# A two-layer decoder trunk on one core: block sums' VectorE steps behind the low parts of probabilities, strided pairs that begin with the first sum

## The chip, the cores and the metric

The kernel runs on one core of a Trainium2 chip. The metric is device time in microseconds (us) for one execution of the whole program; lower is better. The engines are named as the profile names them: PE is TensorE, DVE is VectorE, ACT is ScalarE, POOL is GpSimd, and SP issues the DMAs.

## The reference

Two layers over a sequence of 1024 tokens with 1024 channels, in fp32. Each layer normalises x to h, projects h with one combined matrix, runs two attentions, gates and merges them, and then a gated feed-forward part with a short convolution.

```python
for l in range(DEPTH):                                    # DEPTH = 2
    h = rmsnorm(x, norm1[l])
    ...  # h @ w_in[l]: q, k, v of 12 dilated heads and 4 stick-breaking heads, two gates
    # mixer A, groups (window, dilation) = (128, 1), (512, 4), (2048, 16), 4 heads each:
    scores = einsum('brhnqc,brhnkc->brhnqk', qs, kw) * hd**-0.5 + bias      # ALiBi, causal window
    p = exp(scores - max(scores)); o = einsum('...qk,...kc->...qc', p, vw) / sum(p)
    # mixer B: stick-breaking attention in log space
    x = x + (gate_a * (A @ w_br_a) + gate_b * (B @ w_br_b)) @ w_o[l]
    # then x = x + conv-gated FFN(rmsnorm(x, norm2[l]))
```

## The kernel before, in words

**Two parts for one fp32 value.** Matmuls run on a high and a low part of each operand. `split(hi, lo, src)` casts on ACT (the high part, L129 in the profile) and subtracts on DVE (the low part, L130). A product of two such values is three matmuls: high by high, high by low, low by high. For attention probabilities, `parts` (called with p0, p1 or sb) makes p0h and p0l, with a raised priority in the scheduler. `apply` (L729) multiplies first p0h, then p0l, with v.

**Strided pairs.** Fourteen times per layer, two column blocks of w_in that feed dilated heads and gates (128 columns each) are multiplied with h by Strassen's scheme: fewer block products, of sums of blocks. The halves of h are `H[n][part]`, and `half(n, k)` is four 128x512 blocks of them. Four sums of such blocks are made once per layer: S[1], S[2], S[3] and S[4], each in two parts (t_hi, t_lo; the fourth in the place of a half of h itself, as hh and hl). `block_sums` makes the list of their steps. `first` makes block i of a sum on POOL in three steps (L928, L929, L930); `further` turns the first sum's block into the second's, or that into the fourth's, with two DVE steps (L937, L938); `in_two` splits a block. All sums of one kind pass through one buffer, h_sum, block by block. So the next sum's block i can only be written when the one before it has been split.

A pair's program is `pair_rest.run`. It adds and subtracts the raw blocks of weights on POOL (L1031, L1034, L1037, L1038), makes two parts of each (`piece`: w_hi on ACT, w_lo on DVE), and runs the five remaining products with `seven`, twelve matmuls of 128x512 each (L905 to L907). The other two are run earlier in `ahead`; ACT copies the first of them out of its PSUM bank as q1s (L1000), and SP keeps it in memory, from where it is loaded as u. The five products are w6·S[2], w5·S[1], w7·S[3], w3·half(0,1) and w4·S[4]. They are summed in two PSUM banks, i_a (`pa`) and i_c (`pc`), in the order pa, pc, pa, pc, pa; the two names change banks from pair to pair. A product with `first=False` adds onto what its bank holds. After each product DVE adds the bank to a result u or u5 (L1051, L1056, L1064, L1069, L1077), and this read must be done before the next product is added to the same bank.

**What sets the order.** A queue object `dense` hands out matmuls of dense products between the attention's matmuls at a rate per attention item. Block sums are side jobs: `plan(after, steps)` lists them with the names that must be done (N01s, N11s: the scores of an attention item; plain, 01, v0: products), and `aside` runs one at a time. Before the first strided pair all side jobs left are flushed. Within an engine the order is fixed when the program is built; a scheduler with priorities decides it from the order and the priority in which the code issues.

Of the kernel before, what the change touches and what calls it, by code (L numbers as in the profile page):

```python
# [11 lines left out]
ALU = mybir.AluOpType  # L12
# [30 lines left out]
AHEAD_B = 3  # L43
X_AT = (3, 5, 7, 9)
AHEAD = 200


def f32(ap):
    return ap.bitcast(F32)
# [3 lines left out]
def trunk_kernel(ctx, tc, x, norm1, w_in, b_gate, w_br, w_o, norm2, w_up, conv_w, conv_b, w_down, norm_f, out, depth=None, probe=None):  # L53
    nc = tc.nc
    act, dve, pe, pool = nc.scalar, nc.vector, nc.tensor, nc.gpsimd
# [60 lines left out]
    def bank(tag, name):  # L116
        return ps.tile([P, 512], F32, tag=tag, name=name)
# [9 lines left out]

    def split(hi, lo, src):
        act.copy(hi, src)  # L129
        dve.tensor_tensor(lo, src, f32(hi), ALU.subtract)  # L130


    def weights(src, cols, place=None):
# [61 lines left out]
    class Dense:  # L195
# [30 lines left out]
        def at(self, ahead, f):  # L226
            self.later.setdefault(self.count + ahead, []).append(f)
# [26 lines left out]
        def step(self):  # L254
            while True:
                if self.now is None:
                    self.now, self.nxt = self.nxt or self.choose(), None
                    if self.now is None:
                        return bool(self.later) and self.share()
                    self.ready(self.now, READY)  # L260
                    if self.now[2] and not self.started:
                        while self.side:
                            n = len(self.side)
                            self.aside()
                            assert len(self.side) < n, (self.side, self.done)
# [165 lines left out]
    S, B = {}, {}  # L431
# [161 lines left out]
    def parts(src, n, name):  # L593

        hi, lo = small(name + "h", F32R), small(name + "l", F32R)
        with tc.high_priority(offset=AHEAD):
            split(hi[:, :n], lo[:, :n], src[:, :n])
        return hi, lo

    def fold(dst, o):  # L600
# [310 lines left out]
    def block_sums(made):  # L911


        keep = {"o": made} if made is not None else {}
        S.clear()

        def at(t, i):
            if t == 3 and i < 2:
                if "o" not in keep:
                    keep["o"] = sb.tile([P, 2, HF], F32, tag="ot", name="h_sum2")  # L920
                return keep["o"][:, i, :]
            if "r" not in keep:
                keep["r"] = quarter("h_sum")
            return keep["r"][:, i, :]

        def first(t, a, b, i):
            r, (ah, al), (bh, bl) = at(t, i), a()[i], b()[i]
            pool.tensor_tensor(r, f32(al), f32(bl), ALU.subtract)  # L928
            pool.tensor_tensor(r, r, f32(ah), ALU.add)  # L929
            pool.tensor_tensor(r, r, f32(bh), ALU.subtract)  # L930

        def further(t, a, i):
            if t == 4:

                S[4] = half(0, 0)
            r, (ah, al) = keep["r"][:, i, :], a()[i]
            dve.tensor_tensor(r, f32(ah), r, ALU.subtract)  # L937
            dve.tensor_tensor(r, r, f32(al), ALU.add)  # L938

        def in_two(t, i):  # L940
            if t not in S:
                new_s(t)
            split(*S[t][i], at(t, i))

        b11, b12, b21, b22 = (lambda n=n, k=k: half(n, k) for k in range(2) for n in (1, 0))
        todo = []

        def plan(after, steps):

            for k in range(max(steps) + 1):  # L950
                todo.append((after, lambda fs=steps.get(k, ()): [g() for g in fs]))

        def series(after, t, f, lag, gap):
            steps = {}
            for i in range(4):
                steps.setdefault(i * gap, []).append(lambda i=i: f(i))
                steps.setdefault(i * gap + lag, []).append(lambda i=i: in_two(t, i))
            plan(after, steps)

        def third(i):  # L960
            return lambda: first(3, b22, b12, i)

        def cast(i):
            return lambda: in_two(3, i)

        if made is None:
            plan({"B14"}, {0: [third(0)], 6: [third(1)]})
        plan({"B17"}, {0: [third(2)], 1: [cast(0)], 4: [cast(1)], 6: [third(3)], 9: [cast(2)], 14: [cast(3)]})
        series({"N01s"}, 1, lambda i: first(1, b12, b11, i), 7, 6)
        series({"N11s"}, 2, lambda i: further(2, b22, i), 1, 1)  # L970
        series({"plain", "01", "v0"}, 4, lambda i: further(4, b21, i), 1, 1)
        return todo

    def zeros():
# [36 lines left out]
    def pair_rest(dense, l, offs, put, view, grid, kept):  # L1011
# [13 lines left out]
        def run():  # L1025
# [3 lines left out]
            a11, a12, a21, a22 = (raw[0][:, i, :] for i in range(4))  # L1029
            yield  # L1030
            pool.tensor_tensor(a21, a21, a22, ALU.add)  # L1031
            yield
            yield
            pool.tensor_tensor(a11, a21, a11, ALU.subtract)  # L1034
            w6 = piece(a11)
            yield
            pool.tensor_tensor(a12, a12, a11, ALU.subtract)  # L1037
            pool.tensor_tensor(a11, a22, a11, ALU.subtract)  # L1038
            w5 = piece(a21)
            yield  # L1040
            u = sb.tile([P, T], F32, tag="wr", bufs=NRAW, name="u")
            u1, u2 = u[:, HF:T], u[:, 0:HF]
            nc.sync.dma_start(u1, kept)
# [2 lines left out]
            yield  # L1046
            u5 = small("u5")
            pa, pc = bank("ps", "i_a"), bank("ps", "i_c")
            yield from seven(pa, w6, S[2], True, True)
            r2 = u2  # L1050
            dve.tensor_tensor(view(r2), view(u1), grid(pa), ALU.add)  # L1051
            w3 = piece(a12)
            yield "turn"
            yield
            yield from seven(pc, w5, S[1], True, True)
            dve.tensor_tensor(view(u5), view(u1), grid(pc), ALU.add)  # L1056
            w4 = piece(a22)
            if dense.loads:
                dense.loads.pop(0)()
# [11 lines left out]
            dense.last(1)  # L1071
            yield "turn"
            yield
            for word in seven(pa, w4, S[4], False, True):
                yield "turn"
                yield
# [820 lines left out]
```

## Time and profile before

| | |
|---|---|
| runs shown, median | 2701.96 us (2700.45 to 2702.9, 3 runs) |
| profiled execution | 2703.52 us, of which the profile's span is 2701.8 us |
| busy share of the span | PE 98%, DVE 78%, ACT 49%, POOL 27% |
| granted PE clock, mean | 0.996 |
| HBM | 164 GB/s over the span |

A timeline row is: start, duration, engine, line, operation, output and inputs, shapes. Where a row ends in brackets, the engine was idle so long before it, and the name behind the arrow is what ended that idle time. A row of the list of waits is: engine, first waiting instruction, what it waited for, us in total, times, longest. A row of the windows is: the stretch and its length, busy us and instructions of PE, PE's weight loads, DVE, ACT and POOL, then the granted PE clock, the DMA engines' share and GB/s.

### The profile page before, as it was taken

The numbers are of one execution on the slowest core, as the hardware profiler recorded it, in microseconds if no ns is written. First come the engines' busy times: TensorE is split into PE (matmuls) and PEld (weight loads), VectorE is DVE, ScalarE is ACT, GpSimd is POOL, SyncE is SP. The second block draws the span as 40 slices with busy tenths as digits, with TensorE's granted clock in tenths as the row PEclk, the third lists the DMA queues.
The fourth block names the chain that finished last, engine by engine and source line by source line (L and its number), as shares of the span: only waits on it lengthen the run. The fifth ranks groups of instructions, "written<-read, shape, count | busy, mean of one in ns | idle before, by whom it ended". The sixth has DMA issues, their size and how long they took to land. (4 is left out here: it accounts for less than half of the span.)

```text
span 2701.8 us, 37158 instructions
## 1 busy us (share of the span) xinstructions
PE 2650.5 (98%) x13098; PEld 2226.4 (82%) x13098; DVE 2115.7 (78%) x3170; ACT 1314.3 (49%) x2434; POOL 734.9 (27%) x531
## 2 busy tenths in 40 slices
PE   8999999999999999999999999999999999999999
PEld 7888888888888888888889878888788888888888
DVE  5888876675789988897658887766858888998865
ACT  5656544364455555432335655434635555554225
POOL 2004133222233434321120042332311433343210
PEclk9999999999999999999999999999999999999999
DMA  4134489863235444688401334988732443447963
GB/s 153 28 97 125 132 239 234 205 229 118 82 117 172 141 156 143 222 325 313 167 32 48 102 120 145 254 208 226 234 90 75 151 160 135 170 144 254 333 246 121
DMA packets 399559, 448.88 MB, mean 166 GB/s; under 512 B 22044, under 2 KB 319372, under 8 KB 397836
## 3 DMA queue, kind: packets, MB, share of 16 engines
q1 hardware_dynamic: 399372, 446.49, 51.9%
q8 instruction: 104, 1.70, 0.3%
q14 instruction: 83, 0.68, 0.1%
HBM read 300.61 MB, written 142.67 MB: 164 GB/s over the span
## 5 line engine op out<-in xcount | busy, mean ns | idle before, releaser
L130 DVE TENSOR_TENSOR w_lo<-up_a,w_hi 128x512 fp32r<-128x512 f32 x240 | 236.9, 993 | 22.5 <-ACT w_hi L129 22.5
L129 ACT CAST w_hi<-up_a 128x512 fp32r<-128x512 f32 x240 | 149.4, 623 | 186.0 <-PE u_a L906 45.8
L1651 DVE TENSOR_TENSOR x<-x,d_ps 128x512 f32<-128x512 f32 (+1 forms) x228 | 152.3, 672 | 78.0 <-PE d_ps L1645 77.0
L1382 POOL TENSOR_TENSOR cv<-cv 128x512 f32<-128x512 f32 x88 | 131.9, 1509 | 249.0 <-DVE cv L1377 139.1
L130 DVE TENSOR_TENSOR w_lo<-w_raw,w_hi 128x512 fp32r<-128x512 f32 x176 | 133.9, 763 | 64.9 <-ACT w_hi L129 62.3
L129 ACT CAST w_hi<-w_raw 128x512 fp32r<-128x512 f32 x176 | 109.1, 621 | 130.1 <-PE o_ps L156 60.2
L129 ACT CAST w_hi<-in_a 128x512 fp32r<-128x512 f32 x140 | 86.8, 620 | 148.8 <-PE i_a L906 83.4
L130 DVE TENSOR_TENSOR g<-cv,g 128x512 fp32r<-128x512 f32 x154 | 152.3, 990 | 5.2 <-ACT g L129 2.8
L1643 PE MATMUL d_ps<-gd_in,w_hi 128*128 128x512 f32 (+1 forms) x340 | 130.2, 383 | 1.5 <-ACT w_hi L129 1.2
L1645 PE MATMUL d_ps<-gd_in,w_lo 128*128 128x512 f32 (+1 forms) x340 | 129.8, 382 | 0.0
L1644 PE MATMUL d_ps<-gd_in,w_hi 128*128 128x512 f32 (+1 forms) x340 | 129.7, 382 | 0.0
L905 PE MATMUL u_a<-hh,w_hi 128*128 128x512 f32 x320 | 124.7, 390 | 2.7 <-DVE u L1533 2.7
L906 PE MATMUL u_a<-t_lo,w_hi 128*128 128x512 f32 x320 | 124.5, 389 | 0.0
L907 PE MATMUL u_a<-hh,w_lo 128*128 128x512 f32 x320 | 124.5, 389 | 0.0
L905 PE MATMUL u_a<-t_hi,w_hi 128*128 128x512 f32 x320 | 124.5, 389 | 0.0
L906 PE MATMUL u_a<-hl,w_hi 128*128 128x512 f32 x320 | 124.5, 389 | 0.0
L907 PE MATMUL u_a<-t_hi,w_lo 128*128 128x512 f32 x320 | 124.5, 389 | 0.0
L130 DVE TENSOR_TENSOR w_lo<-in_a,w_hi 128x512 fp32r<-128x512 f32 x140 | 115.6, 826 | 3.8 <-ACT w_hi L129 3.5
L1038 POOL TENSOR_TENSOR in_a<-in_a 128x512 f32<-128x512 f32 x28 | 38.0, 1357 | 281.3 <-DVE w_lo L130 281.3
L1643 PE MATMUL d_ps<-gd_in,wd 128*128 128x512 f32 (+1 forms) x292 | 113.9, 390 | 0.0
L129 ACT CAST g<-cv 128x512 fp32r<-128x512 f32 x154 | 94.9, 616 | 38.1 <-POOL cv L1382 29.3
L1645 PE MATMUL d_ps<-gd_in,wd 128*128 128x512 f32 (+1 forms) x292 | 112.8, 386 | 0.0
(395 smaller groups left out, 8706.3 us busy)
## 6 DMA issues: line engine op xcount, KB each, us to landing
gd<-g SPq DMA_DIRECT2D x154, 512.0 KB, 3.6
gd_in<-gd SPq DMA_DIRECT2D x154, 512.0 KB, 6.2
up_a<-in_w_up_dram SPq DMA_DIRECT2D x80, 512.0 KB, 5.7
in_a<-in_w_in_dram SPq DMA_DIRECT2D x56, 512.0 KB, 5.4
w_raw<-in_w_in_dram SPq DMA_DIRECT2D x104, 256.0 KB, 3.4
t_kq<-tk SPq DMA_DIRECT2D x64, 384.0 KB, 7.6
wd_raw<-in_w_down_dram SPq DMA_DIRECT2D x22, 1024.0 KB, 8.0
gin<-gs SPq DMA_DIRECT2D x32, 512.0 KB, 5.2
```

The lines of the kernel that those rows point to most:

```text
L129: act.copy(hi, src)
L130: dve.tensor_tensor(lo, src, f32(hi), ALU.subtract)
L905: pe.matmul(o, w[0][:, c], rh, start=(first and i == 0), stop=False, skip_group_check=True)
L906: pe.matmul(o, w[0][:, c], rl, start=False, stop=False, skip_group_check=True)
L907: pe.matmul(o, w[1][:, c], rh, start=False, stop=(last and i == 3), skip_group_check=True)
L1038: pool.tensor_tensor(a11, a22, a11, ALU.subtract)
L1382: return lambda: pool.tensor_tensor(dst, a, b, ALU.subtract)
L1643: pe.matmul(o[:, sub], wh[:, c], gh[:, sub], start=(i == 0 and k in (0, 4, 5)), stop=False, skip_group_check=True)
L1644: pe.matmul(o[:, sub], wh[:, c], gl[:, sub], start=False, stop=False, skip_group_check=True)
L1645: pe.matmul(o[:, sub], wl[:, c], gh[:, sub], start=False, stop=(i == m - 1), skip_group_check=True)
L1651: dve.tensor_tensor(x, x, o[:, sub], ALU.add)
```

## The change

1. `parts` remembers the DVE instruction of the latest low part of probabilities. The DVE steps of the block sums (`further`, and the low part in `in_two`) are issued behind it in DVE's order. This is an order alone; no engine waits on another for it.
2. The first and the second sum's steps stand in one plan, after N01s: for block i at step 6i `first`, 6i+7 `in_two` of the first sum, 6i+8 `further` to the second, 6i+10 `in_two` of the second. Before, the second sum followed as a plan of its own after N11s.
3. The fourth sum is no longer flushed ahead of the strided pairs. Its steps stand at 2i and 2i+1, and what is left is flushed ahead of the first pair's last product.
4. A strided pair begins with w5·S[1] into `pc` and goes on with w6·S[2] into `pa`, w7·S[3] into `pa`, w3·half(0,1) into `pc` and w4·S[4] into `pa`. Pieces and POOL's steps are put in that order; POOL's subtraction for w7 comes one step later.

```diff
     def split(hi, lo, src):
         act.copy(hi, src)
-        dve.tensor_tensor(lo, src, f32(hi), ALU.subtract)
+        return dve.tensor_tensor(lo, src, f32(hi), ALU.subtract)
+    mark = {}
+    def behind():
+        return tc.issue_after(mark["low"]) if mark else contextlib.nullcontext()
...
-                        while self.side:
+                        while self.side and self.side[0][0] != LAST_SUM:
...
         with tc.high_priority(offset=AHEAD):
-            split(hi[:, :n], lo[:, :n], src[:, :n])
+            mark["low"] = split(hi[:, :n], lo[:, :n], src[:, :n]).ins
...
-            dve.tensor_tensor(r, f32(ah), r, ALU.subtract)
-            dve.tensor_tensor(r, r, f32(al), ALU.add)
+            with behind():
+                dve.tensor_tensor(r, f32(ah), r, ALU.subtract)
+                dve.tensor_tensor(r, r, f32(al), ALU.add)
...
-            split(*S[t][i], at(t, i))
+            with behind():
+                split(*S[t][i], at(t, i))
...
-        series({"N01s"}, 1, lambda i: first(1, b12, b11, i), 7, 6)
-        series({"N11s"}, 2, lambda i: further(2, b22, i), 1, 1)
-        series({"plain", "01", "v0"}, 4, lambda i: further(4, b21, i), 1, 1)
+        for i in range(4):
+            for k, f in (
+                (0, lambda i=i: first(1, b12, b11, i)),
+                (7, lambda i=i: in_two(1, i)),
+                (8, lambda i=i: further(2, b22, i)),
+                (10, lambda i=i: in_two(2, i)),
+            ):
+                steps.setdefault(6 * i + k, []).append(f)
+        plan({"N01s"}, steps)
...
+        plan(LAST_SUM, steps)
...
             yield
             yield
+            w5 = piece(a21)
             pool.tensor_tensor(a11, a21, a11, ALU.subtract)
+            yield
+            pool.tensor_tensor(a12, a12, a11, ALU.subtract)
             w6 = piece(a11)
             yield
-            pool.tensor_tensor(a12, a12, a11, ALU.subtract)
             pool.tensor_tensor(a11, a22, a11, ALU.subtract)
-            w5 = piece(a21)
-            yield
...
+            yield from seven(pc, w5, S[1], True, True)
+            dve.tensor_tensor(view(u5), view(u1), grid(pc), ALU.add)
+            w3 = piece(a12)
+            yield "turn"
+            yield
             yield from seven(pa, w6, S[2], True, True)
             r2 = u2
             dve.tensor_tensor(view(r2), view(u1), grid(pa), ALU.add)
-            w3 = piece(a12)
-            yield "turn"
-            yield
-            yield from seven(pc, w5, S[1], True, True)
-            dve.tensor_tensor(view(u5), view(u1), grid(pc), ALU.add)
             w4 = piece(a22)
...
+            while dense.side:
+                dense.aside()
             for word in seven(pa, w4, S[4], False, True):
```

The lines of the profile shift: L129 and L130 become L132 and L133, L905 to L907 become L913 to L915, L928 to L930 become L936 to L938, L937 and L938 become L946 and L947, L1000 becomes L1015. POOL's L1031, L1034, L1037 and L1038 become L1046, L1050, L1052 and L1055; the reads of the second and first sum's products, L1051 and L1056, become L1071 and L1065.

First, DVE around the attention item N00 in layer 0, before. t_lo is the low part of a block sum's block, ql that of queries.

```order
340 L130 TENSOR_TENSOR t_lo<-h_sum,t_hi 128x512 x2
341 L130 TENSOR_TENSOR p0l<-t_2899,p0h 128x128
342 L130 TENSOR_TENSOR w_lo<-w_raw,w_hi 128x512
343 L130 TENSOR_TENSOR t_lo<-h_sum,t_hi 128x512 x2
344 L937 TENSOR_TENSOR h_sum<-hh_108,h_sum 128x512 x2
345 L130 TENSOR_TENSOR w_lo<-w_raw,w_hi 128x512
346 L938 TENSOR_TENSOR h_sum<-h_sum,hl_109 128x512
347 L130 TENSOR_TENSOR p0l<-t_2927,p0h 128x512
```

And DVE there now.

```order
337 L133 TENSOR_TENSOR p0l<-t_2870,p0h 128x512
338 L133 TENSOR_TENSOR t_lo<-h_sum,t_hi 128x512
339 L551 SCALAR_TENSOR_TENSOR ql<-q_ps,qt 64x512
340 L552 SCALAR_TENSOR_TENSOR ql<-q_ps,qt 64x512
341 L133 TENSOR_TENSOR w_lo<-w_raw,w_hi 128x512
342 L133 TENSOR_TENSOR p0l<-t_2899,p0h 128x128
343 L133 TENSOR_TENSOR w_lo<-w_raw,w_hi 128x512
344 L133 TENSOR_TENSOR p0l<-t_2927,p0h 128x512
```

The four steps t_lo and the three steps h_sum between the low parts p0l of t_2899 and t_2927 are gone from there; one t_lo stands behind the low part of t_2870.

Second, PE in the third strided pair of layer 0, at the turn from the second product of the pair to the third, before. t_hi_3099 is the first sum, t_hi_2751 the third.

```order
1815 L905 MATMUL i_c_3856<-t_hi_3099,w_hi_3826 128x512
1816 L906 MATMUL i_c_3856<-t_lo_3100,w_hi_3826 128x512
1817 L907 MATMUL i_c_3856<-t_hi_3099,w_lo_3827 128x512
1818 L905 MATMUL i_a_3855<-t_hi_2751,w_hi_3850 128x512
1819 L906 MATMUL i_a_3855<-t_lo_2752,w_hi_3850 128x512
1820 L907 MATMUL i_a_3855<-t_hi_2751,w_lo_3851 128x512
```

And PE there now, where t_hi_3202 is the second sum.

```order
1815 L913 MATMUL i_a_3855<-t_hi_3202,w_hi_3825 128x512
1816 L914 MATMUL i_a_3855<-t_lo_3203,w_hi_3825 128x512
1817 L915 MATMUL i_a_3855<-t_hi_3202,w_lo_3826 128x512
1818 L913 MATMUL i_a_3855<-t_hi_2751,w_hi_3850 128x512
1819 L914 MATMUL i_a_3855<-t_lo_2752,w_hi_3850 128x512
1820 L915 MATMUL i_a_3855<-t_hi_2751,w_lo_3851 128x512
```

The second product of the pair is now the second sum's, and it ends in i_a, the bank in which the third begins.

Third, POOL at the first strided pairs of layer 0, before; in_a_3428 and in_a_3548 are the raw weights of the first and the second pair.

```order
42 L1031 TENSOR_TENSOR in_a_3428<-in_a_3428 128x512
43 L1034 TENSOR_TENSOR in_a_3428<-in_a_3428 128x512
44 L1037 TENSOR_TENSOR in_a_3428<-in_a_3428 128x512
45 L1038 TENSOR_TENSOR in_a_3428<-in_a_3428 128x512
46 L1031 TENSOR_TENSOR in_a_3548<-in_a_3548 128x512
47 L1034 TENSOR_TENSOR in_a_3548<-in_a_3548 128x512
48 L1037 TENSOR_TENSOR in_a_3548<-in_a_3548 128x512
```

And POOL there now, where the two are in_a_3442 and in_a_3532.

```order
39 L1046 TENSOR_TENSOR in_a_3442<-in_a_3442 128x512
40 L1050 TENSOR_TENSOR in_a_3442<-in_a_3442 128x512
41 L1052 TENSOR_TENSOR in_a_3442<-in_a_3442 128x512
42 L936 TENSOR_TENSOR h_sum_2732<-hl0_109,hl1_363 128x512
43 L937 TENSOR_TENSOR h_sum_2732<-h_sum_2732,hh0_108 128x512
44 L938 TENSOR_TENSOR h_sum_2732<-h_sum_2732,hh1_362 128x512
45 L1046 TENSOR_TENSOR in_a_3532<-in_a_3532 128x512
46 L1050 TENSOR_TENSOR in_a_3532<-in_a_3532 128x512
47 L1052 TENSOR_TENSOR in_a_3532<-in_a_3532 128x512
48 L1055 TENSOR_TENSOR in_a_3442<-in_a_3442 128x512
```

The first pair's last step, L1038 before and L1055 now, has moved behind the second pair's three, and the first sum's block 3 behind the first pair's first three. On ACT the cast of the piece made from it, w_hi_3528, stands ahead of the last copy q1s_3445, where it stood behind it before.

More of the change, by code (lines that the diff above doesn't have):

```diff
@@ L1 @@
+import contextlib
 import concourse.bass as bass
@@ L45 @@
 AHEAD = 200
+LAST_SUM = {"plain", "01", "v0"}
 def f32(ap):
@@ L951, in plan @@
                 todo.append((after, lambda fs=steps.get(k, ()): [g() for g in fs]))
[L953 to L958, printed above, removed]
         def third(i):
@@ L968, in block_sums @@
         plan({"B17"}, {0: [third(2)], 1: [cast(0)], 4: [cast(1)], 6: [third(3)], 9: [cast(2)], 14: [cast(3)]})
-        series({"N01s"}, 1, lambda i: first(1, b12, b11, i), 7, 6)
-        series({"N11s"}, 2, lambda i: further(2, b22, i), 1, 1)
-        series({"plain", "01", "v0"}, 4, lambda i: further(4, b21, i), 1, 1)
+        steps = {}
+        for i in range(4):
[7 more added lines that the diff above has]
+        plan({"N01s"}, steps)
+        steps = {}
+        for i in range(4):
+            steps.setdefault(2 * i, []).append(lambda i=i: further(4, b21, i))
+            steps.setdefault(2 * i + 1, []).append(lambda i=i: in_two(4, i))
+        plan(LAST_SUM, steps)
         return todo
```

## The prediction

> **What bounds the kernel now.** The page first. It says that TensorE is the bound.
>
> ```profile
> span 2701.8 us, 37158 instructions
> PE 2650.5 (98%) x13098; PEld 2226.4 (82%) x13098; DVE 2115.7 (78%) x3170; ACT 1314.3 (49%) x2434; POOL 734.9 (27%) x531
> ```
>
> PE is idle for 2701.8 − 2650.5 = 51.3 us in all, so a change that adds no matmul can only move time by taking PE waits away or by adding some. Next I read the list of waits of PE, for the waits that the change can reach.
>
> ```profile
> PE o L729 <- DVE p0l L130: 10.6, 8, 3.1
> PE i_a L905 <- DVE u L1051: 0.6, 1, 0.6
> ```
>
> The first row is the largest wait of the kernel: eight times an apply matmul waits for the low part of probabilities, 5.3 us in each layer. The second is one wait of a strided product for a read of its own PSUM bank; it matters below. The windows show where PE idles.
>
> ```profile
> 240.00:285.00 45.00, 40.66 (x217) 33.71 (x216) 39.85 (x65) 26.15 (x58) 27.95 (x20) 1.00 0.39 117
> 1580.00:1625.00 45.00, 40.63 (x215) 33.66 (x214) 40.69 (x66) 25.78 (x58) 26.32 (x18) 1.00 0.41 124
> ```
>
> PE lacks 4.34 us of 45 in layer 0 and 4.37 in layer 1 (the first pair of figures is PE). The timeline of the first of these stretches shows why (start, duration, both in us).
>
> ```profile
> 265.58 0.57 ACT L129 CAST p0h<-t 128x512 fp32r<-128x512 f32 x1
> 267.05 2.37 DVE L130 TENSOR_TENSOR t_lo<-h_sum,t_hi 128x512 fp32r<-128x512 f32 x2
> 269.35 1.28 DVE L937 TENSOR_TENSOR h_sum<-hh,h_sum 128x512 f32<-128x512 f32 x2
> 271.15 0.68 DVE L938 TENSOR_TENSOR h_sum<-h_sum,hl 128x512 f32<-128x512 f32 x1
> 271.75 0.68 DVE L130 TENSOR_TENSOR p0l<-t,p0h 128x512 fp32r<-128x512 f32 x1
> 269.15 0.28 PE L729 MATMUL o<-p0h,v 128*128 128x256 f32 x1
> 272.49 0.38 PE L729 MATMUL o<-p0l,v 128*128 128x256 f32 x1 [3.06 <-DVE p0l L130]
> ```
>
> The high part stood ready at 265.58 + 0.57 = 266.15, but VectorE works in order, and the block sums' steps stand ahead of p0l.
>
> **Part 1: low parts ahead of the sums.** In the new order p0l stands ahead of those steps, so all 10.6 us can go, and no more, since no other wait there hangs on p0l. What is late next is the chain of the first sum. GpSimd writes the sum of block i into the buffer of which the t_lo of the third sum still has to read block i. That t_lo now stands behind a p0l, so GpSimd starts later, and t_hi of the first sum, which waits for GpSimd, stands on ScalarE ahead of w_hi, qt and the next 512-wide p0h.
>
> ```profile
> 260.61 0.68 DVE L130 TENSOR_TENSOR p0l<-t,p0h 128x512 fp32r<-128x512 f32 x1
> 258.00 1.28 POOL L928 TENSOR_TENSOR h_sum<-hl,hl 128x512 f32<-128x512 f32 x1
> 260.49 1.35 POOL L929 TENSOR_TENSOR h_sum<-h_sum,hh 128x512 f32<-128x512 f32 x1
> 261.92 1.30 POOL L930 TENSOR_TENSOR h_sum<-h_sum,hh 128x512 f32<-128x512 f32 x1
> ```
>
> For block 2: the p0l ends at 261.3, t_lo (0.68) at 262.0, the three GpSimd steps (3.93) at 265.9, then four ScalarE steps of about 0.57 (t_hi, w_hi, qt, p0h) at 268.2, and p0l (0.68) at 268.9. PE without its first wait of 1.28 comes to that matmul's predecessor at 269.15 − 1.28 = 267.9. So about 1.0 of the 4.34 stays; with 0.5 for the smaller p0l and for block 3, which goes the same way, I keep 1.5 per layer, 3.0 in all. The ends are 0 (GpSimd in time) and 5. Part 1: **−10.6 + 3.0 = −7.6** (−10.6 to −5.6).
>
> **Part 2: the strided pairs in the new order.** A pair's five products go to two PSUM banks. Before, the banks alternated: no two products in a row had the same one. Now the second sum's product and the third sum's stand side by side in i_a. The third adds onto what stands in the bank, so its first matmul waits until VectorE (L1071) has read the second's result. This happens once in each of 14 pairs per layer. Nothing else of PE stands between the two in pairs 2 to 5 and 14, four apply matmuls in pair 6, three transposes in 7 and 8, eight score matmuls in 9 to 13. Before, L1056 read the second product of a pair at the same place, with nobody waiting. Its end, set against the start of the third product, is the price. Pair 3 of layer 0 and pair 14 of layer 1 stand for the uncovered ones:
>
> ```profile
> 358.50 0.39 PE L907 MATMUL i_c<-t_hi,w_lo 128*128 128x512 f32 x1
> 358.73 0.39 PE L905 MATMUL i_a<-t_hi,w_hi 128*128 128x512 f32 x1
> 358.93 0.69 DVE L1056 TENSOR_TENSOR u<-u,i_c 128x512 f32<-128x512 f32 x1 [0.55 <-PE i_c L907]
> 1903.67 0.39 PE L905 MATMUL i_a<-t_hi,w_hi 128*128 128x512 f32 x1
> 1904.07 0.68 DVE L1056 TENSOR_TENSOR u<-u,i_c 128x512 f32<-128x512 f32 x1
> ```
>
> The read starts 0.43 after the last matmul's start and ends at 359.62, where the third product had started at 358.73. The one wait of this kind that the trace has gives the hand-over and the restart:
>
> ```profile
> 403.95 0.69 DVE L1051 TENSOR_TENSOR u<-u,i_a 128x512 f32<-128x512 f32 x1 [1.52 <-DMA u<-q]
> 404.70 0.50 PE L905 MATMUL i_a<-t_hi,w_hi 128*128 128x512 f32 x1 [0.58 <-DVE u L1051]
> 405.03 0.39 PE L906 MATMUL i_a<-t_lo,w_hi 128*128 128x512 f32 x1
> 405.03 0.68 DVE L1056 TENSOR_TENSOR u<-u,i_c 128x512 f32<-128x512 f32 x1
> ```
>
> PE starts 0.06 after VectorE's end (404.64), and its second matmul follows after 0.33 in place of 0.23 (358.50 to 358.73), so 0.10 goes for the restart. Pair 3 then waits 359.62 + 0.06 − 358.73 = 0.95 and pair 14 1904.75 + 0.06 − 1903.67 = 1.14: 1.05 on the mean, ten times, 10.5. Pair 6 by the last row: 405.71 + 0.06 − 404.70 = 1.07, twice, 2.1. Pairs 7 and 9 show what cover does:
>
> ```profile
> 426.49 0.69 DVE L1056 TENSOR_TENSOR u<-u,i_c 128x512 f32<-128x512 f32 x1 [0.32 <-PE i_c L907]
> 426.54 0.47 PE L905 MATMUL i_a<-t_hi,w_hi 128*128 128x512 f32 x1
> 462.91 0.69 DVE L1056 TENSOR_TENSOR u<-u,i_c 128x512 f32<-128x512 f32 x1 [0.69 <-PE i_c L907]
> 463.63 0.40 PE L905 MATMUL i_a<-t_hi,w_hi 128*128 128x512 f32 x1
> ```
>
> Behind three transposes 427.24 − 426.54 = 0.70 is left, four times, 2.8; behind eight score matmuls 0.03, ten times, 0.3, which I take as 0.5 for reads that start later. With 16 restarts of 0.10, 1.6: **+17.5** (14.7 with 0.95 each, 0.3 and no restart; 19.0 with 1.2 for each uncovered one, a read that stands behind one more short low part).
>
> The first pair is apart. GpSimd's last subtraction for w7 (L1055) now stands behind the three steps of the next pair's raw weights, and those wait for a DMA. On ScalarE the cast w_hi of w7 waits for it, and behind it stands the copy q1s, which empties the bank that the pair's first product needs.
>
> ```profile
> 318.23 1.63 POOL L1037 TENSOR_TENSOR in_a<-in_a 128x512 f32<-128x512 f32 x1
> 319.26 0.58 ACT L1000 COPY q1s<-r_ps 128x512 f32<-128x512 f32 x1
> 320.36 0.40 PE L905 MATMUL i_a<-t_hi,w_hi 128*128 128x512 f32 x1
> 1656.60 1.63 POOL L1037 TENSOR_TENSOR in_a<-in_a 128x512 f32<-128x512 f32 x1
> 1658.73 0.40 PE L905 MATMUL i_a<-t_hi,w_hi 128*128 128x512 f32 x1
> ```
>
> The next pair's third step ends at 319.86. Then come L1055 (1.30, as GpSimd's other steps above), a cast (0.57), q1s (0.58) and three hand-overs of 0.06: 322.5 against 320.36, and by the same sum 1660.9 against 1658.73. I take 2.15 per layer, **+4.3** (0 if the DMA lands earlier, 5). The DMA follows PE's own work, so I let it move with PE. Last, the first pair's own bank wait: VectorE is crowded there.
>
> ```profile
> 328.67 0.47 PE L905 MATMUL i_a<-t_hi,w_hi 128*128 128x512 f32 x1
> 330.90 0.68 DVE L1056 TENSOR_TENSOR u<-u,i_c 128x512 f32<-128x512 f32 x1
> ```
>
> As it stands that is 331.64 − 328.67 = 2.97; but PE's new stop of 2.15 lets VectorE catch up, down to 0.95 at best. I take 1.5 per layer, **+3.0** (1.9 to 5.9).
>
> GpSimd's late L1055 recurs in pairs 2, 3 and 5, where w7 is needed only at the pair's third product; I take nothing. The fourth sum, no longer flushed, has four products of time; nothing either, as its last block is split before the last product's last quarter. SP's load of u behind the next raw weights: nothing, the first read of u comes a whole product later.
>
> **Sum.** −7.6 + 17.5 + 4.3 + 3.0 = +17.2 on the profiled execution's 2703.52 (span 2701.8 and 1.72 around it), 2720.7. The median of the runs, 2701.96, is 1.56 lower: **2719**. All low ends give −10.6 + 14.7 + 0 + 1.9 = +6.0, 2708; all high ends −5.6 + 19.0 + 5 + 5.9 = +24.3, 2726.
>
> **The rivals.**
>
> *The bank wait is hidden* (the other side). The waits of part 2 cost as little as behind score matmuls, 28 × 0.03 = 0.8, and q1s is in time: −7.6 + 0.8 = −6.8, 2695. It decides at about 0.95 us of PE work between the two products; the eight score matmuls give that (the last matmul starts 0.43 before the read, at 462.48, and 463.63 less its own 0.23 leaves 0.92). For it: ten of 28 pairs have that. Against it: the other 18 have less by the order itself, and ten have nothing. Chance 0.06.
>
> *The change does not do what it says*: p0l stands ahead, but its p0h comes late by the GpSimd chain in both blocks, and the waits stay at 10.6. The sum is +24.8, 2727. For it: the chain above has steps that no trace has shown in this order, and 2 us more on GpSimd or ScalarE bring the long wait back. Against it: by the rows it ends 3.5 before the p0l of now (272.43). Chance 0.13.
>
> *The cheap end*: part 1 is whole, q1s is in time and the first pair's read is prompt: +17.2 − 3.0 − 4.3 − 1.1 = +8.8, 2711. Chance 0.13.
>
> *The clock falls* with so many short stops. The trace has both answers:
>
> ```profile
> 420.45 0.33 PE L590 MATMUL z<-t_kq 128*128 128x128 f32 x1 [1.46 <-DVE st L813]
> 420.00:423.00 3.00, 2.55 (x11) 2.27 (x12) 2.79 (x11) 1.96 (x7) 1.18 (x1) 0.70 1.02 289
> 270.00:274.00 4.00, 1.51 (x8) 1.35 (x9) 4.00 (x8) 1.10 (x2) 0.00 (x0) 1.00 0.36 105
> ```
>
> After a stop of 1.46 us the granted clock was 0.70 on the mean over 3 us, about 0.9 us lost; after one of 3.06 us it stayed at 1.00. If each of the 18 stops of about 1 us cost 0.9, +16 comes on top, 2735. Against it: one stop of 1 us in a pair of five products is little idle time, and the row at 404.70, after a stop of 0.58, is followed by matmuls of 0.39. Chance 0.06. The Trainium skill ("TensorE: Matmul & The Clock Gate", "A second HAM failure mode: psum-queue depth-cycling") speaks for this rival: it tells of a kernel that cycles through banks, whose small idle gaps make the clock go back and forth. By its section "What's actually happening" a whole idle window of about 3.4 us is needed, by which no stop here would cost clock; the row at 420 disagrees with that, the row at 270 doesn't.
>
> **How the numbers follow.** Forecast 0.62, rivals 0.06, 0.13, 0.13 and 0.06. A measurement of this kernel can tell about 0.2%, 5.4 us, from no change. Faster by more than that: 0.05, nearly all of the first rival. Within it: 0.05, its rest and the lowest part of the cheap end. Slower: 0.90. The range 2707 to 2730 holds the forecast with all its bounds, the cheap end and the second rival, with room above for three or four stops that cost clock as at 420; it leaves out the first rival and the last.
>
> **What would show it.** Right: the list of PE's waits has a new row, i_a for u (L1071), about 20 times, 15 to 20 us and the longest 1 to 3, pairs 9 to 13 almost absent; the row o for p0l falls to some 3; the strided pairs' first product waits for q1s some 2 us, once per layer. Wrong: no such row for i_a, or one under 8 us; p0l still at 10; the granted clock under 0.95 over the pairs.

## The result, and the profile after

The changed kernel takes 2743.95 us (median of 5 runs, 2741.65 to 2747.72), against 2701.96 before: a ratio of 1.0155, 95% interval 1.0143 to 1.0167. It is slower by 42 us. The forecast was slower by 17, 2719, in a range of 2707 to 2730; the time lies 14 us above that range.

The page of after, its span and the busy shares:

```profile
span 2742.1 us, 37153 instructions
...
PE 2668.1 (97%) x13098; PEld 2232.3 (81%) x13098; DVE 2096.6 (76%) x3170; ACT 1310.0 (48%) x2434; POOL 733.3 (27%) x531
```

The span grew by 40.3 us. PE's idle time grew from 51.3 to 74.0, which is 22.7. The other 17.6 are in PE's busy time, with the same 13098 matmuls: they were slower. The list of PE's waits, after, names the first part:

```profile
PE i_a L913 <- DVE u L1071: 18.8, 18, 2.8
PE r_ps L163 <- DVE ql L552: 6.5, 4, 1.9
PE o L839 <- DVE p1l L133: 4.7, 8, 0.8
PE o L839 <- ACT p1h L132: 4.6, 5, 2.1
PE i_a L913 <- DVE u L1094: 4.1, 2, 2.2
...
PE i_c L913 <- ACT q1s L1015: 1.9, 2, 1.0
...
PE o L737 <- ACT p0h L132: 0.9, 2, 0.5
PE o L737 <- DVE p0l L133: 0.7, 2, 0.3
```

The wait for p0l fell from 10.6 to 0.7, with 0.9 for p0h beside it. The bank wait came: 18.8 us, 18 times. Three rows were not foreseen: L1094, the read of a pair's fifth product; and p1h and p1l, 1.2 and 1.1 before, now 4.6 and 4.7. The row for ql was 2.7 before.

The slower matmuls show in the windows (the figure after POOL's is the granted clock):

```profile
328.00:332.00 4.00, 3.10 (x11) 2.69 (x12) 4.00 (x9) 0.62 (x1) 0.00 (x0) 0.71 0.91 249
376.00:380.00 4.00, 3.33 (x10) 2.66 (x11) 3.01 (x5) 1.14 (x2) 0.00 (x0) 0.69 0.87 262
1688.00:1692.00 4.00, 4.00 (x14) 3.32 (x13) 3.15 (x6) 0.62 (x1) 0.87 (x1) 0.57 0.58 151
```

In windows of 4 us over the whole span, leaving out the first 20 us and the last 10, after has eight such stretches and before two. Each costs about 1.7 us: 4 us at 0.57 in the third row, 4 x 0.43. So six more stretches, some 10 us, are clock. The rest of the busy time comes with each stop: the last matmul's own end counts as busy (0.39 where the next would have followed after 0.23), and the second matmul behind the stop comes after 0.33. That is about 0.16 + 0.10 = 0.26 for each stop.

The bank wait, in pair 3, where the prediction's rows of before were taken (timeline of after, PE and DVE):

```profile
362.02 0.39 PE L915 MATMUL i_a<-t_hi,w_lo 128*128 128x512 f32 x1
...
362.44 0.69 DVE L1071 TENSOR_TENSOR u<-u,i_a 128x512 f32<-128x512 f32 x1 [0.59 <-PE i_a L915]
...
363.27 0.47 PE L913 MATMUL i_a<-t_hi,w_hi 128*128 128x512 f32 x1 [0.87 <-DVE u L1071]
363.58 0.40 PE L914 MATMUL i_a<-t_lo,w_hi 128*128 128x512 f32 x1
```

The two matmuls stand 1.25 apart in place of 0.23, and the next comes 0.31 later: 1.10 lost, where 0.95 + 0.10 was forecast.

And this is what the forecast took at nothing, the late subtraction for w7, here that of the fourth pair (timeline of after, the engines one after another):

```profile
368.67 1.30 POOL L1046 TENSOR_TENSOR in_a<-in_a 128x512 f32<-128x512 f32 x1 [9.17 <-DMA in_a<-in_w_in_dram]
...
372.66 1.28 POOL L1055 TENSOR_TENSOR in_a<-in_a 128x512 f32<-128x512 f32 x1
...
373.98 0.62 ACT L132 CAST w_hi<-in_a 128x512 fp32r<-128x512 f32 x1 [6.33 <-POOL in_a L1055]
...
374.63 0.69 DVE L133 TENSOR_TENSOR w_lo<-in_a,w_hi 128x512 fp32r<-128x512 f32 x1 [4.93 <-ACT w_hi L132]
...
375.84 0.68 DVE L1094 TENSOR_TENSOR u<-u,i_a 128x512 f32<-128x512 f32 x1
...
374.03 0.39 PE L915 MATMUL i_c<-t_hi,w_lo 128*128 128x512 f32 x1
...
376.67 0.47 PE L913 MATMUL i_a<-t_hi,w_hi 128*128 128x512 f32 x1 [2.25 <-DVE u L1094]
...
378.23 0.63 PE L915 MATMUL i_a<-t_hi,w_lo 128*128 128x512 f32 x1
```

POOL waits for the fifth pair's raw weights, and L1055 stands behind them. ACT is idle for 6.33 us at the cast of w7, DVE for 4.93 at its low part. L1094, the read of the third pair's last product, whose last matmul started at 371.31, stands behind that low part. PE, which needs the bank two products later, waits 2.25, and then runs at 0.63 a matmul.

### The profile page after: what moved, and what is told of

Read it like the earlier page. It is cut to its first block, busy times and chain, and to the rows that moved or that the text cites. A ratio compares the mean times of both kernels' runs of the same rounds, so it can differ in the third digit from the quotient of the medians.

```text
span 2742.1 us, 37153 instructions
## 1 busy us (share of the span) xinstructions
PE 2668.1 (97%) x13098; PEld 2232.3 (81%) x13098; DVE 2096.6 (76%) x3170; ACT 1310.0 (48%) x2434; POOL 733.3 (27%) x531
## 4 chain that ended last, share of the span: by engine, by line
PE 72%; DVE 10%; DMA 3%; POOL 2%; issue 2%; ACT 2%; SPq 0%; DVEq 0%; POOLq 0%; ACTq 0%
PE u_a L913 5%; PE u_a L914 5%; PE u_a L915 5%; PE d_ps L1660 4%; PE d_ps L1661 4%; PE d_ps L1662 4%; PE u_c L914 3%; PE u_c L913 3%; PE u_c L915 3%; PE o_ps L163 2%; PE o_ps L165 2%; PE o_ps L164 2%; PE i_a L913 2%; DVE w_lo L133 2%; DMA in_a<-in_w_in_dram 2%
## 5 line engine op out<-in xcount | busy, mean ns | idle before, releaser
L133 DVE TENSOR_TENSOR w_lo<-up_a,w_hi 128x512 fp32r<-128x512 f32 x240 | 236.8, 993 | 20.0 <-ACT w_hi L132 20.0
L132 ACT CAST w_hi<-up_a 128x512 fp32r<-128x512 f32 x240 | 149.4, 622 | 183.8 <-PE u_a L914 41.6
L133 DVE TENSOR_TENSOR w_lo<-w_raw,w_hi 128x512 fp32r<-128x512 f32 x176 | 132.8, 757 | 68.2 <-ACT w_hi L132 64.6
L132 ACT CAST w_hi<-in_a 128x512 fp32r<-128x512 f32 x140 | 86.6, 619 | 199.7 <-POOL in_a L1055 75.5
L132 ACT CAST w_hi<-w_raw 128x512 fp32r<-128x512 f32 x176 | 109.1, 620 | 126.0 <-PE o_ps L164 62.3
L133 DVE TENSOR_TENSOR g<-cv,g 128x512 fp32r<-128x512 f32 x154 | 152.3, 990 | 5.2 <-ACT g L132 2.8
L133 DVE TENSOR_TENSOR w_lo<-in_a,w_hi 128x512 fp32r<-128x512 f32 x140 | 106.6, 761 | 46.9 <-ACT w_hi L132 46.4
L913 PE MATMUL u_a<-hh,w_hi 128*128 128x512 f32 x320 | 124.7, 390 | 0.2
L915 PE MATMUL u_a<-t_hi,w_lo 128*128 128x512 f32 x320 | 124.5, 389 | 0.0
L915 PE MATMUL u_a<-hh,w_lo 128*128 128x512 f32 x320 | 124.5, 389 | 0.0
L913 PE MATMUL u_a<-t_hi,w_hi 128*128 128x512 f32 x320 | 124.5, 389 | 0.0
L913 PE MATMUL i_a<-t_hi,w_hi 128*128 128x512 f32 x224 | 95.6, 427 | 23.0 <-DVE u L1071 18.8
L132 ACT CAST g<-cv 128x512 fp32r<-128x512 f32 x154 | 94.9, 616 | 38.5 <-POOL cv L1399 29.3
```

What stands on the lines that cost most here:

```text
L133: return dve.tensor_tensor(lo, src, f32(hi), ALU.subtract)
L913: pe.matmul(o, w[0][:, c], rh, start=(first and i == 0), stop=False, skip_group_check=True)
L915: pe.matmul(o, w[1][:, c], rh, start=False, stop=(last and i == 3), skip_group_check=True)
```

## The experiments

Theory A, from the profile after: the loss is in the new order of the strided pairs, by the bank wait and by the late w7; the early part is a gain. Theory B: the sums' new plan and order hold a share of the loss. The runs use the lines of their own files; the text names steps by what they do.

**1. The sums' steps behind the low parts, alone.** To the kernel before only `mark`, `behind()` and its three uses were added.

> The kernel before, with the block sums' VectorE steps ordered behind the last low part of probabilities, and nothing else. Theory A (the loss is in the strided pairs; the early part is a gain): the wait of o for p0l falls from 10.6 to 1-4 us, about 2 us come back as longer waits for ql, and the time is 2694-2699. Theory B (the delayed sums give it all back, by way of GpSimd and ScalarE): p0l and p0h and ql together still hold 10 us or more, and the time is 2700-2706.

It took 2724.73 us, ratio 1.0084 (1.0069 to 1.0099): neither. The p0l wait went to 0.7, but the second sum, which the first pair's first product (in i_a) needs in the old pair order, was late. The list of PE's waits of this run:

```profile
PE r_ps L162 <- DVE ql L551: 6.5, 4, 1.9
PE i_a L913 <- DVE t_lo L132: 5.5, 8, 1.4
PE i_a L912 <- ACT t_hi L131: 4.6, 4, 1.8
```

The rows of i_a are short stops one behind the other in the first pair, and the clock is low over them:

```profile
316.00:340.00 24.00, 17.90 (x63) 12.41 (x61) 21.25 (x34) 10.43 (x20) 1.97 (x2) 0.72 0.06 22
```

24 us at 0.72 are 6.7 us lost. The part of the change that the forecast credited with 7.6 us costs 23 when it stands alone. The merged plan and the later fourth sum are what make it bearable: runs 3 and 8 below have them, with the old pair order, and cost 7.5 us and nothing.

**2. The new pair order, alone.**

```diff
 # the kernel before, with pair_rest of the changed kernel,
 # and without its flush of the fourth sum:
-            while dense.side:
-                dense.aside()
```

> The kernel before, with the new order of products and pieces in the strided pairs, and with the sums planned, ordered and flushed as before. Theory A: nearly all of the loss is here and none of the gain: a row i_a for u (second product's read) of 17-24 us, a row for the fourth product's read of about 4 us, four to six more stretches of low clock at 1.7 us each; 2740-2755. Theory B: only the bank wait of about 20-25 us: 2722-2728.

2750.23 us (2741.29 to 2757.13), ratio 1.0176 (1.0151 to 1.0201): as A expected, the loss and none of the gain. Its runs differ by 16 us, more than any other kernel's here.

```profile
PE i_a L905 <- DVE u L1056: 17.5, 18, 2.7
PE o L729 <- DVE p0l L130: 10.4, 7, 3.1
PE o L831 <- ACT p1h L129: 5.9, 5, 2.2
PE o L831 <- DVE p1l L130: 5.0, 9, 0.8
...
PE i_a L905 <- DVE u L1077: 3.6, 2, 1.8
```

Bank wait, fifth product's read (L1077 here), p1h and p1l are all there. So the p1 rows, too, come from the pair order. The last section comes back to the spread.

**3. The changed kernel with the old pair order.** `run` as before, with the late flush kept.

> The changed kernel, with the strided pairs' products, pieces and GpSimd steps back in the order of before; the sums' plan, their order on VectorE and the late flush of the fourth sum stay as changed. Theory A: no row i_a for a second product's read, at most 0.6 us; 2692-2701. Theory B: the merged plan and the late fourth sum hold a share of the loss: 2710-2725.

2709.24 us, ratio 1.0029 (1.0017 to 1.0040): between the two. No bank wait, but the first pair's last product waits 7.5 us for hh, the late fourth sum, and 6.5 us (2.7 before) to ql.

**4. w7 one step earlier.** The subtraction put right behind `w6 = piece(a11)`, ahead of the `yield`.

> The changed kernel, with GpSimd's subtraction for w7 one step earlier, right behind the piece w6 and so ahead of the next pair's raw weights. Theory A (VectorE's low part of w7 waits for it and holds back the read of the fourth product behind it): the row i_a for the fourth product's read falls from 4.1 us to under 0.5, the first product's wait for q1s from 1.9 to under 0.5, and two stretches of low clock go: 9-12 us less, 2732-2736. Theory B (that read is late for another reason): 2742-2746 with the rows unchanged. The row of 18.8 us for the second product's read stays in both.

2747.28 us, ratio 1.0160 (1.0145 to 1.0176). This run tells nothing on w7: the scheduler left the order on POOL as it was.

**5. w7 ordered ahead of the next raw weights.** The order is now forced.

```diff
-            pool.tensor_tensor(a21, a21, a22, ALU.add)
+            with tc.issue_after(mark["w7"]) if "w7" in mark else contextlib.nullcontext():
+                pool.tensor_tensor(a21, a21, a22, ALU.add)
...
-            pool.tensor_tensor(a11, a22, a11, ALU.subtract)
+            mark["w7"] = pool.tensor_tensor(a11, a22, a11, ALU.subtract).ins
```

> The changed kernel, with GpSimd's first step on a pair's raw weights ordered behind the subtraction for w7 of the pair before. (The edit of the run before, one step earlier in the code, left GpSimd's order as it was, so it tested nothing.) Theory A: late w7 blocks ScalarE and VectorE, and what stands behind it there is late: the fourth product's read 4.1 us goes under 0.5, q1s 1.9 under 0.5, p1h and p1l together from 9.3 to 2-4, two or three stretches of low clock go; the bank wait of 18-19 us stays: 2726-2733. Theory B (the late w7 is harmless, those waits come from elsewhere): 2740-2746.

2727.40 us, ratio 1.0099 (1.0082 to 1.0116): 16.6 less than the changed kernel (16.2 when each is set against the kernel before, measured beside it), as A expected. The rows of L1094, q1s and p1h are out of the list, p1l is at 1.5; the bank wait stays:

```profile
PE i_a L913 <- DVE u L1072: 20.2, 17, 3.2
PE r_ps L163 <- DVE ql L552: 6.5, 4, 1.9
```

**6 and 7. Banks that alternate.** The third, fourth and fifth product go to the other bank, once without and once with the order of run 5. These kernels compute other sums, so they price an order and can't be used.

```diff
-            pa, pc = bank("ps", "i_a"), bank("ps", "i_c")
+            pc, pa = bank("ps", "i_c"), bank("ps", "i_a")
...
-            yield from seven(pa, w7, S[3], False, True)
+            yield from seven(pc, w7, S[3], False, True)
...
-            yield from seven(pc, w3, half(0, 1), False, True)
+            yield from seven(pa, w3, half(0, 1), False, True)
...
-            for word in seven(pa, w4, S[4], False, True):
+            for word in seven(pc, w4, S[4], False, True):
```

> The changed kernel, with the third, fourth and fifth product of a strided pair in the other bank each, so that no two products in a row share one. It adds the third to the first product's bank and so computes other sums; every instruction stays, in number and size. Theory A: the row for the second product's read falls from 18.8 us to under 1, the restarts (18 times 0.26) and the low clock that follow it go, the rows of w7 stay: 2714-2722. Theory C (VectorE is late anyway, and the wait only moves to the next product): 2730-2740.

> Both edits of the two runs before, other sums as there. Theory A: what is left is the early part's gain of 9 us, less about 4 us of longer waits for ql and one stretch of low clock per layer: 2697-2706. Theory B or C, or a third cost that neither edit touches: 2710 or more.

2736.59 us (2728.65 to 2743.49), ratio 1.0128 (1.0104 to 1.0152), and 2715.54, ratio 1.0054 (1.0039 to 1.0069). Both miss A's range, and C has the first one's number. The bank row is gone in both, but a wait takes part of its place: not for DVE's reads but for the late fourth sum, hh 10.7 us in the first, hh 5.5 and hl 3.5 in the second. So in the changed kernel the bank waits hide a late fourth sum, and part of what they cost would be lost without them too.

**8. Old pair order, and the fourth sum early.** Run 3 with the flush ahead of the first pair's second product.

> The changed kernel with the strided pairs in the order of before (the run at 2709), and the fourth sum's steps flushed ahead of the first pair's second product in place of its last. Theory A: the wait of the first pair's last product for hh (7.5 us, twice 3.8) falls under 1 and one stretch of low clock per layer goes: 2696-2701. Theory B (the fourth sum's steps then delay other work of VectorE by as much): 2705-2710.

2701.26 us, ratio 1.0001 (0.9991 to 1.0010): the time of before, just above A's range. The hh row is gone. So the whole part on the sums, put as well as this, brings nothing, though p0l and p0h together hold 4.2 us in place of the 10.6 of p0l. ql holds 6.5:

```profile
PE r_ps L163 <- DVE ql L552: 6.5, 4, 1.9
PE o L737 <- ACT p0h L132: 3.0, 4, 1.1
...
PE o L737 <- DVE p0l L133: 1.2, 4, 0.3
```

**9. The new pair order alone, with w7 ordered.** Run 2 with the edit of run 5.

> The kernel before with the new order of the strided pairs alone (the run at 2750), and GpSimd's first step on a pair's raw weights ordered behind the subtraction for w7 of the pair before. Theory A: only the bank wait is left of the 48 us, 17-20 us in the list, 18 restarts of 0.26 and at most one stretch of low clock more: 2724-2731, with the p0l row back at about 10. Theory B (the new order costs more than these two): 2738 or more.

2727.38 us, ratio 1.0090 (1.0075 to 1.0105), against 2703.04 beside it: A's time. What is left of 48 us is 24, and the bank wait is its one large row:

```profile
PE i_a L909 <- DVE u L1061: 19.4, 18, 2.7
PE o L733 <- DVE p0l L134: 10.1, 6, 3.1
```

19.4 us and 18 stops of 0.26, 4.7, make 24.1. That this meets the measured 24.3 is luck in part: the run has three more stretches of low clock than the kernel before, 5 us in all, where A allowed one stretch, and its other waits are about 5 us shorter. Nor was the bank wait alone taken out here; the row names it. Run 7 takes it out on top of run 5, and run 10 with the fourth sum early besides: they are 12 and 17 us faster than run 5 (each against the kernel before beside it), with other waits in its place.

**10. Alternating banks, w7 ordered, the fourth sum early.**

> The run with alternating banks and ordered w7 (2715.5; other sums, as there), with the fourth sum flushed ahead of the first pair's second product. Theory A (its remainder was the late fourth sum: hh 5.5 and hl 3.5 us and low clock behind them): those two rows go under 1 and the time comes to that of the run with the old pair order and the early fourth sum, 2698-2705. Theory B (something else of the new order still costs): 2708 or more.

2711.69 us, ratio 1.0032 (1.0017 to 1.0046): hh and hl are gone, but a new row stands there, 5.5 us for the second product's read in the first pair (twice 2.7), for which the fourth product waits, as the flush puts the fourth sum's DVE steps ahead of it. It is B's time, but the flush itself brings the new row, so the run is no clean price of the bank wait.

**11. Queries at a high priority.** Run 8, with qt and ql issued like the probabilities' parts.

> The kernel with the old pair order and the early fourth sum (2701.3), with the queries' two parts issued at the priority of the probabilities' parts. Theory A (the early gain of 9 us is given back there: t_hi of the first sum waits for GpSimd on ScalarE ahead of qt, and PE's next product waits for ql to empty its bank, 6.5 us in all, with low clock behind it): the row r_ps for ql falls from 6.5 to under 3, p0h from 3.0 to under 2: 2692-2698, 4-9 us faster than the kernel before. Theory B (another step on VectorE is late then): 2699-2704.

2711.31 us, ratio 1.0032 (1.0020 to 1.0044): neither. The ql row fell to 1.8, but p0h rose to 12.3. On ACT it stands behind both qt, 0.6 us more than in run 8, and, with them, behind a t_hi of the first sum that waited 7.73 us for POOL, against 2.97 in run 8. For POOL's order moved too: two steps of a strided pair (L1050, L1053) now stand between the three of that sum (timeline of this run):

```profile
267.48 1.25 POOL L939 TENSOR_TENSOR h_sum<-h_sum,hh 128x512 f32<-128x512 f32 x1
...
268.77 0.62 ACT L132 CAST t_hi<-h_sum 128x512 fp32r<-128x512 f32 x1 [7.73 <-POOL h_sum L939]
```

So this run doesn't tell what early queries alone are worth.

**12. The third sum's low parts free.** Run 8, where `in_two(3, i)` is no longer behind the low parts.

```diff
-            with behind():
+            with contextlib.nullcontext() if t == 3 else behind():
                 split(*S[t][i], at(t, i))
```

> The kernel with the old pair order and the early fourth sum (2701.3), where the third sum's low parts are no longer ordered behind the probabilities' low parts; those of the other sums still are. Theory A (the early gain is given back because GpSimd waits for that t_lo, and t_hi of the first sum then blocks ScalarE ahead of qt and p0h): the idle time of ScalarE there goes, o for p0h and p0l and r_ps for ql fall from 10.7 us together to 3-5, no low clock behind them: 2692-2698. Theory B (VectorE has too much to do there in any order): 2699-2704, with the waits moved to the sums' products in the first pair.

2701.33 us, ratio 0.9996 (0.9987 to 1.0005): no change. ACT no longer waits for POOL there, yet ql still holds 6.4 us. It is B's time, but the waits didn't move to the sums' products, as B had it.

**13 and 14. The queries' low part ahead of the next p0l.** Run 12, and the kernel before as a control, with this edit.

```diff
+        with tc.high_priority(offset=AHEAD):
             dve.scalar_tensor_tensor(la[0:64], o[0:64], scale, f32(qa[0:64]), ALU.mult, ALU.subtract)
             dve.scalar_tensor_tensor(lb[64:128], o[64:128], scale, f32(qb[64:128]), ALU.mult, ALU.subtract)
```

> The run before (third sum's low parts free, old pair order, early fourth sum), with the two VectorE steps of the queries' low part issued at the priority of the probabilities' parts, so that both stand ahead of the next on and p0l. Theory A (this wait takes the early gain): r_ps for ql falls from 6.4 to 2-4 us, one stretch of low clock per layer goes with it, p0h and p0l stay at 4 together: 2693-2698. Theory B (VectorE is full there, and p0l is late in its place): p0l up by as much, 2699-2704.

> The kernel before with that edit of the queries' low part alone. Theory A: the p0l wait of 10.6 us hides this one there, so little happens: 2699-2703, with r_ps for ql at 1-3 us and p0l at 10-11. Theory B: 2695 or less, and then a gain of the run beside it is not the change's.

2695.47 us, ratio 0.9974 (0.9964 to 0.9984), and 2704.21, ratio 1.0012 (1.0003 to 1.0021). The first, in A's range, is the fastest kernel of this study, 5.7 us under the 2701.16 of before beside it. The second lies just above A's range, with ql at 3.9: the edit gains nothing by itself. The first one's list of waits:

```profile
PE r_ps L163 <- DVE ql L553: 4.3, 4, 1.4
...
PE o L738 <- ACT p0h L132: 2.2, 2, 1.1
...
PE o L738 <- DVE p0l L133: 1.7, 4, 0.6
```

The ql row fell by 2.1 only. Run 12's two stretches of low clock behind that wait, one in each layer, are gone here; at 1.7 us each they are most of the rest.

## Why the prediction was wrong

The direction, and the mechanism that was given the most weight, were right. Three terms of the sum were not. Nor was the premise that a change which adds no matmul moves time by PE's waits alone: 17.6 of the span's 40.3 us are in PE's busy time.

**Late w7, taken at nothing: 16.6 us.** The step that failed is the sentence on L1055 "in pairs 2, 3 and 5, where w7 is needed only at the pair's third product; I take nothing". It asked only when PE needs w7. It didn't ask what stands behind w7's cast on ACT and its low part on DVE, in engines that work in order: the fifth product's read of the pair before, p1h, p1l. Its count was off as well. In the trace of after L1055 stands behind the next pair's three steps in pairs 1, 2, 4 and 10 to 13 of each layer; before, L1038 stood ahead of them in all fourteen. All five of PE's waits for p1h are in pairs 10 to 13; here it is pair 10's w7 (timeline of after):

```profile
484.40 1.29 POOL L1055 TENSOR_TENSOR in_a<-in_a 128x512 f32<-128x512 f32 x1
...
485.73 0.62 ACT L132 CAST w_hi<-in_a 128x512 fp32r<-128x512 f32 x1 [6.58 <-POOL in_a L1055]
486.25 0.85 ACT L132 CAST p1h<-t 128x384 fp32r<-128x384 f32 x2
...
486.77 0.38 PE L839 MATMUL o<-p1h,t_v 128*128 128x256 f32 x1 [1.10 <-ACT p1h L132]
```

In the first pair the same was asked (q1s), and found: 1.9 us where 4.3 was forecast. The chain is the one forecast (L1055 ends at 317.30, PE goes on at 318.49); the next pair's raw weights came earlier against PE than in the kernel before. By runs 5 and 9 against after and run 2, this mechanism, q1s included, is 16.6 us in the changed kernel and about 23 in the new pair order alone (run 2's spread makes this figure rough).

**Bank wait, 20.5 forecast, 23.5 by the rows of after.** Pairs 2 to 14: the list's 18.8 less the two first pairs (2.79 and 2.80) is 13.2 over 16 stops, with 0.26 each 17.4, against 17.5. So close a sum is luck in part. The ten turns with nothing between stopped PE for 0.87 to 1.10 us and once for 1.75, 13.2 with the 0.26 each, against 11.5; pairs 6 to 8, partly covered, for 0.37 to 0.45, 4.2 against 5.5; pairs 9 to 13 not at all. The first pair cost 2.8 + 0.26 each, 6.1, against 3.0. The prediction let VectorE catch up there, and it didn't: low parts and the fourth sum's steps stand ahead of the read. That holds in run 9 too, with the sums as before and 2.7 us.

```profile
327.56 0.68 DVE L946 TENSOR_TENSOR h_sum<-hh,h_sum 128x512 f32<-128x512 f32 x1
328.16 0.68 DVE L1071 TENSOR_TENSOR u<-u,i_a 128x512 f32<-128x512 f32 x1
...
328.89 0.50 PE L913 MATMUL i_a<-t_hi,w_hi 128*128 128x512 f32 x1 [2.79 <-DVE u L1071]
```

**Early part, −7.6 forecast, about 0 measured** (runs 5 and 9, with and without the sums' changes, are 25.8 and 24.3 us over the kernel before beside them, with overlapping intervals; run 8 has the time of before). The p0h and p0l waits fell as forecast, even lower (0.9 and 0.7). What was missed is the next bank: PE's r_ps product waits until DVE has read q_ps. In after, its timeline on DVE and PE:

```profile
266.71 0.69 DVE L133 TENSOR_TENSOR p0l<-t,p0h 128x512 fp32r<-128x512 f32 x1 [0.26 <-ACT p0h L132]
...
268.55 0.54 DVE L133 TENSOR_TENSOR p0l<-t,p0h 128x384 fp32r<-128x384 f32 x1
269.12 0.69 DVE L552 SCALAR_TENSOR_TENSOR ql<-q_ps,qt 64x512 fp32r<-64x512 f32 x1
...
269.96 0.47 PE L163 MATMUL r_ps<-hh,w_hi 128*128 128x512 f32 x1 [1.87 <-DVE ql L552]
```

Another p0l stands ahead of ql. The wrong step is "no other wait there hangs on p0l". The prediction's own chain, by way of POOL, is real: ACT sat idle for 2.98 us there. But run 12 took it away and gained nothing; only with the ql order of run 13 does the time fall. Both have the old pair order; in the changed kernel itself the ql order was not tried. And it took back only 2.1 of the 3.8 us by which the ql row had grown.

So −7.6 for the early part, 20.5 for the bank wait and 4.3 for late w7 were forecast, and about 0, 24.3 (run 9) and 16.6 (run 5) measured: 40.9 of the 42. As differences between runs these add up almost by construction; what bears them out is that runs 5 and 9 agree. The fourth sum, taken at nothing, waits for 1.0 us in after (hl), but for 7.5 and 10.7 us (hh) in runs 3 and 6, without the bank waits.

**The rivals.** The hidden bank wait is refuted by the 18 waits of after and by run 9. "The change does not do what it says" is not borne out: p0h and p0l hold 1.6 us, not 10.6, and the gain is gone by another way. The cheap end had none of its three conditions whole. The falling clock was given 0.06 and is there, at a smaller size: six more stretches of 1.7 us, 10 us of the 42 where that rival had 16, no cost of its own but an addition to each of the others. The prediction's price of 0.9 for one fall came from a window of 3 us that ends inside the stretch. Its sign, under 0.95 over the pairs, was too coarse: over them the clock was 0.99 and 0.98. Seven of the eight falls stand behind stops of 1.8 to 2.8 us. The eighth, at 1380, follows a stop of 0.95 and 0.9 us of matmuls of one column each, and whether these are its cause was not tested. Behind the 16 shorter bank stops the clock stayed at 1.00. The Trainium skill ("TensorE: Matmul & The Clock Gate", "A second HAM failure mode: psum-queue depth-cycling") was cited for that rival, and the trace agrees with it in part: the clock did fall and rise again behind small idle gaps, but mostly behind single stops of 1.8 us and more, and not behind the 16 turns from product to product in one bank that the change put into pairs 2 to 14.

## What to carry to other kernels

When a step is made late, follow each engine's queue behind it, and not only the product that uses its result: a cast that waits on ACT or DVE holds back the reads that empty other banks. When a wait on the path is removed, look for the next bank that PE takes, and who empties it. An order of products that adds twice in a row to one bank costs the read between them, a stop of 0.9 to 1.1 us here at most places; three transposes between left 0.45 of it, eight score matmuls nothing.

## What the runs showed of the hardware

A stop of PE well under 3 us can lower its clock for the next few microseconds: after one of 2.25 us matmuls took 0.63 in place of 0.39 (row at 378.23), and the two windows from 376 to 384 lose 1.7 us. It doesn't always: in after, PE's stop of 1.88 for ql in layer 1 (at 1627.05) has windows of 4 us at 0.85 and 0.73 behind it, and that of 1.87 in layer 0 (at 269.96) has 1.00. The stop of 3.06 us before p0l in the kernel before left the clock at 1.00, and the same stop in run 2, again 3.06 (at 273.28), stands in a window of 4 us at 0.53:

```profile
272.00:276.00 4.00, 2.72 (x8) 2.34 (x9) 3.94 (x8) 0.62 (x2) 0.00 (x0) 0.53 0.51 164
```

Run 2's times spread over 16 us, and its profile, the slowest of its four runs, has eleven such stretches. The mean granted clock of each run is on record, and it falls as the time rises: 0.997 at 2741.29 us, 0.995 at 2746.36, 0.992 at 2754.09 and at 2757.13. A mean lower by 0.005 over 2750 us is, by estimate, 14 us, so most of the spread goes with the clock. What makes the clock fall in one run and not in another stays open.
